# A transformer block with three branches on one core: TensorE's list tied to the order of the source

## The chip, the cores and the metric

The kernel runs on one core of one Trainium2 chip. A core has five engines with a list of instructions each: TensorE (PE; its weight loads are shown as PEld), VectorE (DVE), ScalarE (ACT), GpSimd (POOL) and SyncE (SP), which issues most transfers. The metric is device microseconds of one execution of the program, as the median of several runs.

## The reference

One block over 512 tokens of 1,024 channels, in float32. A modulation of `c` scales and shifts both norms and gates both residuals. The first half projects the normed input to three mixing branches of 512 channels and to three gates:

```python
mod = cond @ w_ada[l] + b_ada[l]
h = rms_norm(x) * norm1_g[l] * (1.0 + sc1) + sh1
proj = h @ w_in[l]
...
y_fox = fox_attention(...)      # softmax attention with a decay from cumulative log gates
y_hgrn = hgrn2_branch(...)      # linear attention with data-dependent decay, chunks of 64
y_rwkv = rwkv7_branch(...)      # delta rule: state S, then S*w - (S k)(k a) + v k, token by token
merged = (g_fox * (y_fox @ w_branch[l, 0]) + g_hgrn * (y_hgrn @ w_branch[l, 1])
          + g_rwkv * (y_rwkv @ w_branch[l, 2]))
x = x + gt1 * (merged @ w_out[l])
h = rms_norm(x) * norm2_g[l] * (1.0 + sc2) + sh2
u = causal_dwconv(h @ w_up[l], conv_w[l], conv_b[l])
x = x + gt2 * ((silu(u_gate) * u_val) @ w_down[l])
```

## The kernel before, in words

**Stages.** The kernel has a start (first modulation parts, the first norm, the first tiles of `w_in`), an interleaved part (all projections, the three branches, the gates and the merge), the output product with the second norm, and the FFN (`w_up`, convolution, `w_down`).

**Large products.** Each float32 weight tile is split into a high and a low part, and a product is three matmuls of the type float32r (`mm3`, L348): high x high, high x low, low x high. `load` (L337 for the transfer) fetches 256 KB, and `split` puts the high part on ScalarE (L329) and the low part on VectorE or GpSimd (L330). The raw tiles have 3 buffers, the parts 6 each. A product's output has one of 3 PSUM banks (`mm`), the branches' small products share 5 more (`br`).

**Streams.** In the interleaved part seven generators take turns, in this order of precedence: `rwkv_b`, `rwkv_a`, `hgrn`, `foxes`, `prep`, `ada_stream` and `big`. Each branch works in four groups of two heads. `big` is a list of jobs with the large weights, one `mm3` for each of eight blocks of rows between two yields. A step of a stream ends with `yield lat`. The planner `run` keeps a clock, `clk`, that counts an estimated TensorE time for each matmul and transpose from its shape alone, and a stream may go on when `clk` has passed its last `lat` times 0.9, plus 1.65. At each turn the first stream in the list that is due makes its next step; `need` and `post` hand results from one stream to another with a due time. So the source's order of matmuls follows from shapes and from these constants.

**The framework's order.** The kernel is written in a framework that works out tiles' places, semaphores and each engine's list by itself. It goes through the traced instructions with a model of time: an instruction is put on its engine's list when the model has its operands and buffers ready, earlier ones of the source first among those that are ready. So an instruction that the model holds to be late is overtaken by later ones. Each engine then runs its list in order. `tc.issue_after(ins)` says that what is traced in the block comes behind `ins` on the same engine's list; it orders the issue and does not wait for the end of `ins`. Two accesses to one PSUM tile by different engines, one of them a write, are ordered by semaphores even where the columns differ.

**The places that matter here.**
- `rwkv_b` (L985 on) is a chain over 8 chunks for each of the four groups, in one PSUM tile per chunk. A chunk has three steps: the product with `G` and `MV` (columns 0 to 63) and its copy `xst` (L1001); the product of `Z64` and `xst` (64 to 127) and `UV` from it (L1010); and the last step, in which, for c < 7, the product `BT x UV` (128 to 191) is read by two VectorE instructions into the next `MV` (L1020, in chunk 0 L1023), and then the output products `AR x MV` and `G x UV` (192 to 255) are read by ScalarE (L1031).

```python
            if c < 7:
                for hh in range(2):
                    mm(ps[HS[hh], 128:192], BT[hh][:, c, :], uv[:, hh, :])
...
                for hh in range(2):
                    hs = HS[hh]
                    if c > 0:
                        v.scalar_tensor_tensor(out=mvn[hs, hh, :], in0=ps[hs, 128:192], scalar=wc[hs, c:c + 1],
                                               in1=xst[hs, cl, 1, :], op0=ALU.mult, op1=ALU.add)
...
            for hh in range(2):
                hs = HS[hh]
                o = ps[hs, 192:256]
                if c > 0:
                    mm(o, AR[hf][hs, cl, 1, :], mv[hs, hh, :], True, False)
                mm(o, G[hh][hf][:, cl, 64:128], uv[:, hh, :], c == 0, True)
```

- `split2` (L465 ScalarE, L466 VectorE) makes two parts `shi` and `slo` of a float32 tile. `rwkv_a` calls it in the head of the loop that multiplies both by `bonesr` (four times), and `ada_stream` in the one that multiplies both by `onesr` (four times).
- `rwkv_a` waits for a spread reciprocal norm `rnx` (L438) before four transposes, and multiplies `AR` by `BK` in four groups of four.
- `fox_decay` makes the first product of the interleaved part (tile `wf`).
- `transpose` and `mm` are the two helpers that every stream calls; most matmuls therefore have L88 and most transposes L92.

Of the kernel before, what the change touches and what calls it, by code (L numbers as in the profile page):

```python
# [42 lines left out]
def block_kernel(ctx: ExitStack, tc: tile.TileContext, I, out, dbg=None, upto=99):  # L43
# [32 lines left out]

    # the work of the branches is cut in steps, which the streams below interleave; the clock counts the work of the
    # tensor engine, and a step says after how much of it the operands of the next are expected
    clk = [0.0]

    def mm(o, lhsT, rhs, start=True, stop=True):
        n = rhs.free_size() if hasattr(rhs, "free_size") else math.prod(rhs.shape[1:])
        if rhs.dtype == F32R:
            clk[0] += n / 2400
        else:
            half = (0.5 if lhsT.shape[0] <= 64 else 1.0) * (0.25 if math.prod(lhsT.shape[1:]) <= 32 else 1.0)
            clk[0] += half * max(0.17, n / 600)
        return pe.matmul(o, lhsT=lhsT, rhs=rhs, start=start, stop=stop)  # L88

    def transpose(o, i, idn):  # L90
        clk[0] += 0.11 if i.shape[0] > 64 else 0.07
        pe.transpose(o, i, idn)  # L92

# [14 lines left out]
    def run(streams):  # L108
        """streams in the order of their precedence"""
        live = [[gen, 0.0, False] for gen in streams]  # L110
        while live:
            done = False
            for st in live:
                if st[1] > clk[0] + 1e-9:
                    continue
                c0, n0 = clk[0], len(avail)
                try:
                    lat = next(st[0])
                except StopIteration:
                    live.remove(st)  # L120
                    done = True
                    break
                if lat is None and c0 == clk[0] and n0 == len(avail):
                    continue
                lat = lat or 0.0
                st[1] = clk[0] + (lat * LAT[0] + LAT[1] if lat else 0.0)
                done = True
                break
            if not done:
                later = [st[1] for st in live if st[1] > clk[0] + 1e-9]  # L130
                assert later, "streams wait for each other"
                clk[0] = min(later)
# [16 lines left out]

    # ---------------------------------------------------------------- constants  # L150
    con = cp.tile([P, NCONST], F32, name="con")
    lmask = cp.tile([P, 5, 64], I32, name="lmask")
    last = {}

    def behind(key, emit):
        """an instruction queued behind the one before with the same key"""
        if key in last:
            with tc.issue_after(last[key]):
                r = emit()
        else:  # L160
            r = emit()
        last[key] = r.ins
        return r
# [49 lines left out]

    # ---------------------------------------------------------------- x, modulation
    modc = cp.tile([P, 48], F32, name="modc")
# [57 lines left out]

    # ---------------------------------------------------------------- norm helpers
    def rstd_of(ss, n, eps, dst, w):
# [24 lines left out]
    def normed(xs):  # L300
        """the normed halves of a tile of 128 tokens"""
        return norm_scale(xs, norm_stats(xs))
# [18 lines left out]

    # ---------------------------------------------------------------- weights
    nld = [0]
# [20 lines left out]
    def load8(src, c0):  # L344
        """1024 x 128 of a weight, in two halves; the parts of each block of 128 rows"""
        return load4(src, c0, 0) + load4(src, c0, 1)
# [5 lines left out]

    # the first tiles of w_in take the first half of the channels while the second is on its way
    ALLT = list(range(4))
# [54 lines left out]
    def chunk_tokens(src, dst):  # L409
        """channels x tokens to tokens x channels: chunks of 64 tokens, odd heads in the other half of the partitions;  # L410
        dst(hh, par) takes the chunks 2 * i + par"""
        ps = PSB()
# [8 lines left out]
    def chunk_channels(src):  # L421
        """the inverse of chunk_tokens: (head, parity of the chunk, [64 channels, 4 chunks, 64 tokens])"""
        ps = PSB()
# [17 lines left out]
    def head_bcast(rnx):  # L441
        """[128 tokens, (tile, head)] to a PSUM bank [128 channels, 512 tokens]"""
        psr = PSB()
# [4 lines left out]
    def head_sums(sqs, sums=None):  # L448
        """of each [128 channels, 512 tokens] the sums over the channels of a head, as [128 tokens, (tile, head)]"""
        n = len(sqs) * P  # L450
# [17 lines left out]

    # ================================================================ HGRN
    lbm = small("lbm", [P, 4])  # L470
# [11 lines left out]
    def hgrn(gi):  # L482
# [23 lines left out]
        for li, m in enumerate(LEVELS):  # L506
            ps = PSB()
            for c in range(8):
                for hh in range(2):
                    if m == 32:  # L510
                        # the lower half of the chunk against the upper one only
                        qq = Q[2 * hh + c % 2]
# [20 lines left out]
        vi, = yield from need(("hi", gi))  # L533
        # [A; q] and [V; state] of each head, odd heads with the halves exchanged: one product takes both
        VM = [T2("VM", [P, 8, 64]) for _ in range(2)]
# [64 lines left out]

    # ================================================================ FOX
    ncum = dp.tile([6, 8, 512], F32, name="ncum")
# [6 lines left out]
    def fox_decay():  # L609
# [23 lines left out]
        v.tensor_tensor_scan(out=cum, data0=one, data1=z, initial=0.0, op0=ALU.mult, op1=ALU.add)  # L633
        # the sum in three parts, and their negatives
        for i in range(3):
# [14 lines left out]
    def fox(gi):  # L650
# [9 lines left out]
        g.tensor_tensor(out=rn, in0=rn, in1=as3(neghalf[:, 0:16], 8), op=ALU.pow)  # L660
        # [high; low] of q against [high; high] of k (odd heads: [low; high]), and high of q against low of k with the
        # parts of the sums of both tokens
        A = [[T2("qk1", dt=F32R) for _ in range(2)] for _ in range(2)]
# [81 lines left out]

    # ================================================================ RWKV
    w2s = []
# [29 lines left out]
    def rwkv_evac(n, j, ps):  # L777
# [11 lines left out]
        if n == "rwa":  # L789
            # [high; low] parts, for products with [high; high] and with the low part of the weights  # L790
            ll = []
# [20 lines left out]
    def rwkv_a(gi):  # L812
# [64 lines left out]

        # products of all pairs of steps in a chunk, for both heads
        G, BT = [[None, None], [None, None]], []
        Ld = T2("Ld", [P, 8, 64])  # L880
        for hf in range(2):
            for hh in range(2):
# [7 lines left out]
                yield 0.0  # L890
        # inverses of the 16 x 16 diagonal blocks, one system (chunk, head, block) per partition
        d1 = dp.tile([8 * 8320], F32, tag="d1", bufs=2, name=nm("d1"))
# [34 lines left out]
        for x in range(2):  # L927
            sync.dma_start(d2[x].rearrange("(s e) -> s e", e=256), XZ[:, x].rearrange("p i j -> p (i j)"))
            sync.dma_start(Xc[:, x], dview(d2, x * 8 * 2048, [[16, 128], [2048, 8], [1, 16]]))
        # [U; V] and [state; V] of each chunk: odd heads have the halves exchanged  # L930
        UV = [T2("UV", [P, 4, 2, 64]) for _ in range(2)]
# [44 lines left out]
        for hh in range(2):  # L976
            v.tensor_scalar(out=Z64[Q[2 * hh], :, 32:64], in0=ps[Q[2 * hh], 0:256].rearrange("p (c j) -> p c j", j=32),
                            scalar1=-1.0, scalar2=0.0, op0=ALU.mult, op1=ALU.add)
            for hf in range(2):
                # the rows of the inverted block give way to alpha: one product then takes the state and V  # L980
                s.activation(G[hh][hf][HS[hh], :, 0:64], AR[hf][HS[hh], :, 0, :], AF.Copy)
# [3 lines left out]
    def rwkv_b(gi):  # L985
# [47 lines left out]
        post(("chained", gi), None)  # L1033
        # group norm over the 64 channels of each head
        sm = small("gsum", [P, 8])
# [26 lines left out]

    # ================================================================ products with the large weights
    gt1 = [T2("gt1") for _ in range(2)]
# [74 lines left out]
    def ada_stream():  # L1139
        """the rest of the modulation, on engines that have time left"""  # L1140
        yield 100.0
# [80 lines left out]
    def foxes():  # L1222
        yield from fox_decay()
        yield from each(fox)

    run([each(rwkv_b), each(rwkv_a), each(hgrn), foxes(), prep(), ada_stream(), big(jobs)])

# [53 lines left out]

    # ================================================================ FFN
    cw_rows = T2("cw_rows", [44, 4, 128])
# [13 lines left out]

    # the first tiles start with the first half of the tokens, while the norm of the second is worked out
    begun = []
# [39 lines left out]
    for k in range(KT):  # L1339
        for q in range(2):  # L1340
            w = load(w_down, k * P, P, q * 512, 512)
            for tt in range(4):
                down_mm(k, q, tt, w)
    # the last rows tile by tile, so that the tiles are done one after the other
    ws = [[load(w_down, k * P, P, q * 512, 512) for k in range(KT, 22)] for q in range(2)]
# [9 lines left out]

# [1 line left out]
def _constants(np):  # L1357
# [5 lines left out]
    m = np.where(rho, sp <= tp, sp < tp).astype(np.float64)  # L1363
    # without the products of the steps of a block of 16, whose inverse is worked out apart
    off = (i[:, None] % 64) // 16 != (i[None, :] % 64) // 16
# [45 lines left out]
```

## Time and profile before

| what | us |
|---|---|
| median of 3 runs | 1149.66 |
| the 3 runs | 1149.66, 1147.6, 1160.29 |
| the profiled execution | 1160.29 |
| its span, from the first to the last instruction | 1158.6 |
| TensorE busy in the span | 1111.0 (96%) |
| VectorE, ScalarE, GpSimd busy | 697.9, 520.8, 302.7 |

The profile is of one execution. Start times are microseconds from the span's first instruction. Matmuls are pipelined, so that one 128x512 matmul shows some 0.39 us though the next one starts 0.23 us after it; what counts is the distance between starts. A float32 matmul shows as two records, so the count of a small product in a row is twice that in the source. "Idle before" stands in square brackets with what ended it.

### The profile page before, as it was taken

What the parts mean: (1) busy time and instruction counts of PE and PEld (TensorE: products, weight loads), DVE (VectorE), ACT (ScalarE), POOL (GpSimd) and SP (SyncE); (2) the same over time, 40 slices, a digit from 0 to 9 for tenths busy, and PEclk for the clock granted to TensorE, in tenths of its full rate; (3) what the DMA queues carried; (4) which work ended last, traced back from release to release, by engine and by line L of the source; (5) the groups of instructions that cost most, each with busy time, mean ns of one, the idle gap of its engine ahead of it and who ended that gap; (6) DMA issues with size and microseconds to landing.
All of it is one profiled execution on the core that took longest, in us unless ns stands there. A gap on an engine that the chain in (4) does not pass through costs nothing. (4 is left out here: it accounts for less than half of the span.)

```text
span 1158.6 us, 19335 instructions
## 1 busy us (share of the span) xinstructions
PE 1111.0 (96%) x7297; PEld 858.9 (74%) x7297; DVE 697.9 (60%) x1477; ACT 520.8 (45%) x975; POOL 302.7 (26%) x322
## 2 busy tenths in 40 slices
PE   4998999999999999999999999899999999999998
PEld 2567876777777776677767888688888888888886
DVE  1567668777688778676653824735666666661114
ACT  2475575256535653568432434323444444442220
POOL 3015424323343234231131622432101101101110
PEclk9999999899999998999989999899999999999999
DMA  9633352133412413143524455301333333333332
GB/s 312 200 77 78 79 141 57 40 107 77 129 31 85 118 48 112 38 110 101 154 56 127 112 178 173 119 1 32 109 98 95 99 95 98 99 94 97 100 98 84
DMA packets 175475, 117.60 MB, mean 102 GB/s; under 512 B 25360, under 2 KB 151350, under 8 KB 175382
## 3 DMA queue, kind: packets, MB, share of 16 engines
q1 hardware_dynamic: 173696, 116.22, 35.0%
q8 instruction: 57, 0.93, 0.3%
q14 instruction: 36, 0.29, 0.1%
q10 hardware_dynamic: 1238, 0.12, 0.1%
q0 software_dynamic: 448, 0.03, 0.0%
HBM read 112.57 MB, written 3.77 MB: 100 GB/s over the span
## 5 line engine op out<-in xcount | busy, mean ns | idle before, releaser
L329 ACT ACTIVATE whi<-raw 128x512 fp32r<-128x512 f32 x282 | 176.1, 629 | 351.9 <-PE mm L88 230.3
L330 DVE TENSOR_TENSOR wlo<-raw,whi 128x512 fp32r<-128x512 f32 x212 | 151.4, 715 | 153.1 <-ACT whi L329 152.2
L330 POOL TENSOR_TENSOR wlo<-raw,whi 128x512 fp32r<-128x512 f32 x70 | 94.9, 1355 | 460.3 <-ACT whi L329 436.0
L88 PE MATMUL mm<-hhi,whi 128*128 128x512 f32 x504 | 212.5, 422 | 0.3 <-DVE rwa L780 0.3
L88 PE MATMUL mm<-hhi,wlo 128*128 128x512 f32 x504 | 202.6, 402 | 0.0
L88 PE MATMUL mm<-hlo,whi 128*128 128x512 f32 x504 | 202.2, 401 | 0.0
L88 PE MATMUL mm<-h2hlo,whi 128*128 128x512 f32 (+1 forms) x376 | 141.5, 377 | 1.2 <-POOL h2hlo L1261 1.2
L88 PE MATMUL mm<-h2hhi,whi 128*128 128x512 f32 (+1 forms) x376 | 141.3, 376 | 0.0
L88 PE MATMUL mm<-h2hhi,wlo 128*128 128x512 f32 (+1 forms) x376 | 141.2, 376 | 0.0
L88 PEld LDWEIGHTS mm<-hhi,whi 128*128 128x128 f32 x504 | 96.7, 192 | 24.0 <-issue 2.0
L88 PEld LDWEIGHTS mm<-hhi,wlo 128*128 128x128 f32 x504 | 96.5, 191 | 21.7 <-issue 0.4
L88 PEld LDWEIGHTS mm<-hlo,whi 128*128 128x128 f32 x504 | 96.7, 192 | 16.7 <-issue 0.4
L88 PEld LDWEIGHTS mm<-h2hlo,whi 128*128 128x128 f32 x376 | 70.7, 188 | 14.7 <-POOL h2hlo L1261 2.0
L88 PEld LDWEIGHTS mm<-h2hhi,wlo 128*128 128x128 f32 x376 | 70.7, 188 | 12.9
L88 PEld LDWEIGHTS mm<-h2hhi,whi 128*128 128x128 f32 x376 | 70.7, 188 | 12.9
L1319 DVE SCALAR_TENSOR_TENSOR u<-mm,cw,u 128x511 f32<-128x511 f32 x44 | 32.8, 746 | 54.7 <-ACT u L1318 54.7
L1150 DVE SCALAR_TENSOR_TENSOR adac<-ada,cs,adac 128x512 f32<-128x512 f32 x56 | 45.1, 805 | 0.7
L1004 POOL TENSOR_SCALAR xst<-MV,wc 64x64 f32<-64x64 f32 x48 | 20.8, 434 | 93.7 <-DVE MV L1020 86.0
L88 PE MATMUL br<-wlo,ahi 128*128 128x512 f32 x110 | 42.8, 389 | 0.0
L88 PE MATMUL br<-whi,alo 128*128 128x512 f32 x110 | 42.8, 389 | 0.0
L88 PE MATMUL br<-whi,ahi 128*128 128x512 f32 x110 | 42.8, 389 | 0.0
L88 PE MATMUL mm<-yhi,whi 128*128 128x512 f32 x96 | 38.7, 404 | 0.7 <-DVE gt L1130 0.7
(385 smaller groups left out, 2026.4 us busy)
## 6 DMA issues: line engine op xcount, KB each, us to landing
raw<-in_w_in_dram SPq DMA_DIRECT2D x126, 256.0 KB
ada<-in_w_ada_dram SPq DMA_DIRECT2D x96, 256.0 KB
raw<-in_w_up_dram SPq DMA_DIRECT2D x88, 256.0 KB
raw<-in_w_down_dram SPq DMA_DIRECT2D x44, 256.0 KB
raw<-in_w_branch_dram SPq DMA_DIRECT2D x24, 256.0 KB
wo<-in_w_out_dram SPq DMA_DIRECT2D x16, 256.0 KB
x<-in_x_dram SPq DMA_DIRECT2D x8, 256.0 KB
mg<-in_x_dram SPq DMA_DIRECT2D x8, 256.0 KB
```

The lines of the kernel that those rows point to most:

```text
L88: return pe.matmul(o, lhsT=lhsT, rhs=rhs, start=start, stop=stop)
L329: s.activation(hi, raw, AF.Copy)
L330: (g if leng == "g" else v).tensor_tensor(out=lo, in0=raw, in1=hi.bitcast(F32), op=ALU.subtract)
L1004: g.tensor_scalar(out=xst[HS[hh], cl, 1, :], in0=mv[HS[hh], hh, :], scalar1=wc[HS[hh], c:c + 1], scalar2=0.0, op0=ALU.mult, op1=ALU.add)
L1150: v.scalar_tensor_tensor(out=acc, in0=raws[k], scalar=cs[:, k:k + 1], in1=acc, op0=ALU.mult, op1=ALU.add)
L1319: v.scalar_tensor_tensor(out=u[:, 1:], in0=ps[:, :511], scalar=cw[:, 1, jj:jj + 1], in1=u[:, 1:], op0=ALU.mult, op1=ALU.add)
```

## The change

`mm` and `transpose` pass their instruction through `in_order`, which remembers the last one and, once the flag `strict` is set, traces the next inside `tc.issue_after` of it. The flag is set right before the interleaved part starts and isn't set back, so the products of `w_out` and the FFN that go through `mm` are tied too; the transposes of the norms (L311) and of the convolution's weights call `pe.transpose` directly and are not. Apart from that the diff removes comments, which moves the line numbers.

```diff
+    pe_last = [None]
+
+    def in_order(emit):
+
+        if pe_last[0] is None or not strict[0]:
+            r = emit()
+        else:
+            with tc.issue_after(pe_last[0]):
+                r = emit()
+        pe_last[0] = r.ins
+        return r
+
+    strict = [False]
...
     def mm(o, lhsT, rhs, start=True, stop=True):
...
-        return pe.matmul(o, lhsT=lhsT, rhs=rhs, start=start, stop=stop)
+        return in_order(lambda: pe.matmul(o, lhsT=lhsT, rhs=rhs, start=start, stop=stop))
 
     def transpose(o, i, idn):
         clk[0] += 0.11 if i.shape[0] > 64 else 0.07
-        pe.transpose(o, i, idn)
+        in_order(lambda: pe.transpose(o, i, idn))
...
+    strict[0] = True
     run([each(rwkv_b), each(rwkv_a), each(hgrn), foxes(), prep(), ada_stream(), big(jobs)])
```

## Rows read from the trace of the kernel before

**Rows 1.** The page's busy times of the whole span, with shares and counts.
```profile
PE 1111.0 (96%) x7297; PEld 858.9 (74%) x7297; DVE 697.9 (60%) x1477; ACT 520.8 (45%) x975; POOL 302.7 (26%) x322
```

**Rows 2.** Busy us by stretch: PE, PEld, DVE, ACT, POOL (x instructions), clock, DMA share, GB/s.
```profile
54.40:736.00 681.60, 659.80 (x5228) 495.72 (x5228) 465.04 (x1100) 348.96 (x678) 226.65 (x234) 0.97 0.36 98
811.00:1141.00 330.00, 330.00 (x1457) 273.05 (x1456) 166.81 (x244) 127.14 (x207) 38.80 (x30) 1.00 0.33 96
```

**Rows 3.** TensorE's waits: us in total, times, longest us.
```profile
PE br L88 <- POOL pr L492: 3.0, 1, 3.0
...
PE br L88 <- DVE MV L1020: 2.3, 2, 1.7
```

**Rows 4.** The tile MV: ns min/median/max, first and last start.
```profile
L1020 DVE SCALAR_TENSOR_TENSOR MV<-br,wc,xst x48: 265/284/292, 199.3 to 625.7; 64x64 f32<-64x64 f32 x48
...
L1023 DVE TENSOR_SCALAR MV<-br,wc x8: 249/284/292, 190.3 to 559.7; 64x64 f32<-64x64 f32 x8
```

**Rows 5.** Timeline from 245.9 us: start, us, engine, line, operation, tiles, count.
```profile
246.03 0.28 PE L88 MATMUL br<-UV,BT 128*64 128x64 f32 x4
...
246.25 0.91 PE L88 MATMUL br<-VM,ktok 64*64 64x64 f32 x22
246.43 0.60 DVE L1020 SCALAR_TENSOR_TENSOR MV<-br,wc,xst 64x64 f32<-64x64 f32 x2 [2.12 <-PE br L88]
...
247.09 0.33 PE L88 MATMUL br<-MV,AR 64*64 64x64 f32 x2
```

**Rows 6.** Timeline, TensorE and VectorE, at 188.9 and at 589 us.
```profile
188.93 0.34 PE L88 MATMUL br<-UV,BT 128*64 128x64 f32 x4
...
190.31 0.57 DVE L1023 TENSOR_SCALAR MV<-br,wc 64x64 f32<-64x64 f32 x2
...
589.42 0.34 PE L88 MATMUL br<-UV,BT 128*64 128x64 f32 x4
...
592.15 0.60 DVE L1020 SCALAR_TENSOR_TENSOR MV<-br,wc,xst 64x64 f32<-64x64 f32 x2
```

**Rows 7.** TensorE's timeline at 101 and 463 us; L466's VectorE instructions.
```profile
101.42 0.40 PE L88 MATMUL mm<-hhi,whi 128*128 128x512 f32 x1
...
109.39 0.49 PE L88 MATMUL br<-slo,bonesr 128*128 128x512 f32 x1
...
463.26 0.80 PE L88 MATMUL mm<-hhi,whi 128*128 128x512 f32 x1
...
471.80 0.50 PE L88 MATMUL br<-slo,bonesr 128*128 128x512 f32 x1
...
L466 DVE TENSOR_TENSOR slo<-rk,shi x4: 681/686/874, 108.4 to 471.0; 128x512 fp32r<-128x512 f32 x4
```

**Rows 8.** TensorE's timeline from 80 us, with the idle time before the last.
```profile
80.61 0.39 PE L88 MATMUL mm<-hhi,whi 128*128 128x512 f32 x1
...
84.46 0.39 PE L88 MATMUL mm<-hhi,wlo 128*128 128x512 f32 x1
86.17 0.66 PE L92 MATMUL br<-con,rnx 128*128 128x128 f32 x4 [1.32 <-DVE rnx L438]
```

**Rows 9.** TensorE's timeline from 92 us.
```profile
92.14 0.39 PE L88 MATMUL mm<-hhi,whi 128*128 128x512 f32 x1
...
94.67 2.82 PE L88 MATMUL br<-AR,BK 64*128 64x128 f32 x32
```

**Rows 10.** Busy us by stretch around stalls, with the granted clock (columns as in rows 2).
```profile
208.50:210.70 2.20, 0.03 (x3) 0.03 (x2) 2.13 (x6) 0.14 (x1) 0.70 (x1) 1.00 0.00 0
210.90:221.10 10.20, 10.20 (x78) 8.26 (x75) 5.65 (x12) 1.84 (x5) 1.47 (x3) 0.50 0.19 30
453.30:466.90 13.60, 13.04 (x79) 9.76 (x80) 8.48 (x23) 5.04 (x14) 1.95 (x4) 0.50 0.17 26
593.20:600.00 6.80, 6.80 (x22) 4.82 (x22) 1.18 (x3) 0.85 (x2) 0.46 (x1) 0.50 0.16 41
```

## The prediction

> **What bounds the kernel now.** I read the page's busy shares first, then the busy times by stretch, then TensorE's list of waits, then the timeline at the places that the change touches. TensorE is busy for 96% of the span, VectorE for 60% [rows 1]. From its first instruction of the interleaved part at 54.4 us to the last at 736 us TensorE is busy 659.80 of 681.60 us: 21.8 us are idle [rows 2]. VectorE has 465 us of work there, so no other engine comes near. The longest single wait in the part's list is 3.0 us, for POOL's `pr`; two for VectorE's `MV` make 2.3 together [rows 3]. So the part ends when TensorE has got through its list. Its work is the same before and after the change: the time moves only by idle time that is added or taken away, and by the clock.
>
> What keeps idle time so low is the framework's reordering. Setting the order that the planner's source gives beside the order in the trace, about 1,100 of some 3,700 matmuls and transposes of the part stand elsewhere, most by under 30 places, one by 116. Nearly always it is one pattern: a small product whose operand is late is overtaken by the three-product groups of a large weight. After the change nothing overtakes, so TensorE stands where it now fills.
>
> **The change, part by part.** It removes and adds no instruction, and it orders issue without waiting for an end. Everything behind the waiting matmul on TensorE's list waits with it: the other streams' small products, the large weights' groups, and through these the splits on ScalarE that need a weight buffer back and the next weight loads on SP's queue. None of these is late by itself; they get TensorE's delay.
>
> *Chain steps of `rwkv_b`.* In each of the steps c < 7 the source has the product `BT x UV` into columns 128 to 192 of a PSUM tile, two VectorE instructions that read them (L1020, or L1023 in step 0), and at once, without a yield, the output products into columns 192 to 256 of the same tile. 48 and 8 VectorE instructions, two a step, make 28 places [rows 4]. The output products need only `UV`, which is there, but they wait for `MV`: the list has two such waits, the longer 1.7 us [rows 3], at the places where too little else stood ready. Where VectorE is free, the `BT` product starts at 246.03, `MV` takes 246.43 to 247.03, the output products start at 247.09; in between TensorE did 11 products of another stream, from 246.25 on [rows 5]. Without these it would stand from 246.25 to 247.09, 0.84 us. 28 x 0.84 = 23.5 us. That is the floor of this term, as an instruction on VectorE can't be skipped.
>
> In ten of the 28 places VectorE comes late, 0.9 to 4.6 us after the `BT` product, the first at 190.31 behind a row of scans, the last at 592.15 behind two `adac` updates [rows 6]; together 20.5 us, or 19.5 over the prompt case. With TensorE standing, less new work reaches VectorE, but chains like these scans go on. I take 6, with 0 and 19.5 as the ends.
>
> *Products of parts just split* (L904, L1161). `split2` is called in the loop's head, with ScalarE and VectorE work and the product of it in one step. For `bonesr` the trace has four such, and TensorE did other things from the source's place to the second part's product: 101.42 to 109.39 in the first, 463.26 to 471.80 in the last [rows 7], 5 to 6 us in the two between. For `onesr` three of four are delayed, by 1 to 4 us. All of it would be 33 us. Most will not come: ScalarE's `shi` stood behind weight splits that waited for large products, which now stand behind `bonesr`, so the framework must put `shi` first. What then remains is one activation and one subtraction; the subtraction takes 0.69 us [rows 7], so some 1.4 us for both if nothing is done ahead. 7 x 1.4 = 10 at most, 0 if both parts are done in time; I take 8.
>
> *The first streams.* From 80.61 to 84.69 TensorE did 18 large products ahead of the transposes of `rnx`, and stood for 1.32 us all the same [rows 8]: 4.1 us more of standing. From 92.14 ten more overtook the products `AR x BK` until 94.67 [rows 9]: 2.3 us. Together 6.4; the decay product of `fox`, 20 places earlier in the source's order, brings its VectorE work forward, so `rnx` may come sooner. I take 5, ends 0 and 6.4.
>
> *The rest of the overtaking*, around 320 to 360 and 460 to 490 us, fills places between chain steps. I take 2, ends 0 and 7: at most 29 large products stand ahead of their place there, at 0.23 us each (17 steps from 80.61 to 84.46 [rows 8]).
>
> *The clock.* TensorE was idle from 208.5 to 210.7, and then the granted clock was 0.50, that is 1.2 of 2.4 GHz, for 10.2 us; the same level follows stalls at 453.3 for 13.6 us and at 593.2 for 6.8 us [rows 10]. Half of each is lost, 15.3 us in all now. Standing under a microsecond at a time need not bring it; the long ones above may. One more such stretch costs 3.4 to 6.8. I take +4, ends -15 and +25.
>
> *Absorbed.* While TensorE stands at a new place, the engines that cause the 21.8 us of present idle time run ahead. I take 8 of it as gone, ends 0 and 17.
>
> Sum: 23.5 + 6 + 8 + 5 + 2 + 4 - 8 = 40.5 us. The terms are from one execution, 1160.29 us with a span of 1158.6; it is the slowest of the three shown, and 10.6 over their median. The sum for it is 1200.8; set on the median of 1149.66 it is 1190 us. FFN and the output product are tied too, as the flag is not set back, but the trace's order there is the source's almost throughout, and I count nothing.
>
> The Trainium skill (Perfetto Trace Analysis, Identifying the Most-Contended Engine) speaks against reading the bound from matmul busy time: it would have the busy share of the weight loads looked at. That share is 72.7% in the interleaved part against 82.7% in a stretch of FFN [rows 2], so by this rule TensorE has a tenth of the part to spare, and the delays could vanish in it. That is the second rival below; the small products load narrower weights, so I don't read the whole difference as room.
>
> **The rivals.**
> 1. *Faster: the present stalls go.* If the source's order, which was planned for operands in time, avoids the stalls after which the clock halves, the most to win is 21.8 us of idle time [rows 2] and 15.3 us of clock [rows 10]; a third of it, with nothing new to pay, gives 1137. It decides if the 28 places cost under 0.3 us each. Against it: `MV` alone takes 0.60 us at each [rows 5], and the stall at 208.5 stands where the order hardly differs.
> 2. *No change: TensorE has slack.* The new standing replaces the old, and the engines behind it catch up: 23.5 less 17 and less one half-clock stretch gives 1151. For it: the weight loads' share. Against it: the late operands depend on TensorE's own earlier products, so they move along.
> 3. *The change hardly does anything*, as seven in ten products are in place already. It would show as 28 places still filled; 1150. The source ties each one to the one before, so I see no way.
> 4. *Much slower: the clock breaks.* VectorE late at all ten places, half the 33 us of the split parts, and four or five more half-clock stretches: 43 + 17 + 6 + 10 + 20 - 5 = 91, so 1241.
>
> **How the numbers follow.** The forecast, slower by 16 to 80 us, has 0.77; rival 1 0.04; rivals 2 and 3 together 0.10; rival 4 0.09. A change under 1%, 11.5 us, is about what a measurement can't tell from none. The low end: 23.5 + 4 + 3 - 14 = 16.5, so 1166. The high end: 43 + 12 + 6 + 6 + 18 - 5 = 80, so 1230. Faster 0.04, within 1% 0.10, slower 0.86.
>
> **What would show it.** In the profile after: the list of TensorE's waits led by VectorE's `MV`, some 28 of them, 0.7 us or more each and 23 to 43 us in total; waits for `slo` and `rnx`; idle time of 55 to 80 us in the part in place of 21.8; the busy time of FFN unchanged; VectorE's busy time unchanged. It is wrong if the waits for `MV` total under 12 us, if the part's idle time does not grow, or if the growth sits in half-clock stretches and not in waits.

## The result and the profile after

The changed kernel takes 1221.64 us (median of 4 runs, 1218.75 to 1222.82) against 1152.94 us for the kernel before (4 runs on the same chip, 1147.6 to 1160.29): a ratio of 1.0566, 95% interval 1.0519 to 1.0612. It is 68.7 us slower by the medians. The two profiled executions, on which the accounting below rests, differ by less, since the one of before was the slowest of its four: their spans are 1219.3 and 1158.6 us, 60.7 us apart.

The page's busy times after, to be set beside [rows 1]:

```profile
PE 1125.8 (92%) x7297; PEld 874.6 (72%) x7297; DVE 697.1 (57%) x1477; ACT 520.6 (43%) x974; POOL 299.3 (25%) x322
```

TensorE issues the same 7297 matmuls, and no other engine has more work. TensorE's share fell from 96 to 92%, and its busy time rose by 14.8 us, though nothing was added to its list. So the loss has two parts: idle time, and the same work done more slowly.

The busy times by stretch show where, with the columns of [rows 2]. The first line is the interleaved part, from the same first instruction at 54.4 us to the same last one, now at 795.0 us; the second is a stretch of FFN.

```profile
54.40:795.00 740.60, 674.07 (x5203) 511.59 (x5201) 462.16 (x1092) 347.65 (x676) 223.16 (x234) 0.93 0.33 90
870.00:1200.00 330.00, 329.89 (x1460) 273.03 (x1459) 167.02 (x244) 128.25 (x208) 39.06 (x31) 1.00 0.33 97
```

The part grew from 681.6 to 740.6 us, by 59.0; only 1.7 of the 60.7 us lie outside it. Of the 59.0, 44.7 us is idle time (740.60 less 674.07 is 66.5; it was 21.8), and 14.3 us is busy time (674.07 less 659.80). The mean granted clock of the part fell from 0.97 to 0.93. FFN is as it was.

TensorE's waits after (us in total, times, longest us) answer to [rows 3]:

```profile
PE br L102 <- DVE MV L1034: 37.2, 24, 6.1
...
PE br L106 <- DVE rnx L452: 4.2, 3, 2.1
PE br L102 <- DVE MV L1037: 4.0, 4, 1.7
PE br L102 <- DVE slo L480: 3.7, 5, 1.5
...
PE br L102 <- POOL pr L506: 3.0, 1, 3.0
PE br L102 <- DVE UV L1024: 2.4, 2, 1.9
PE br L102 <- ACT shi L479: 2.3, 2, 1.5
```

`MV` leads with 24 and 4 waits, 28 in all and 41.2 us, where it had two and 2.3 us. `slo` and `shi` are new, with 6.0 us. Three lines of before that are not in [rows 3] show what changed little or went:

```profile
PE br L92 <- DVE rnx L438: 3.2, 3, 1.4
...
PE br L88 <- DVE mx L707: 2.0, 1, 2.0
PE br L88 <- POOL qk L686: 1.9, 3, 1.0
```

`rnx` rose by 1.0 us, `mx` left the list, `pr` and `UV` stand as they stood.

The next two fences are timelines after (start, us, engine, line, operation, tiles, count, idle time before and what ended it). The first is a place at which VectorE is free, to be set beside [rows 5]; the second is the longest wait.

```profile
268.31 0.28 PE L102 MATMUL br<-UV,BT 128*64 128x64 f32 x4
...
268.71 0.60 DVE L1034 SCALAR_TENSOR_TENSOR MV<-br,wc,xst 64x64 f32<-64x64 f32 x2 [3.02 <-PE br L102]
...
269.37 0.33 PE L102 MATMUL br<-MV,AR 64*64 64x64 f32 x2 [0.77 <-DVE MV L1034]
```

```profile
393.30 0.63 PE L102 MATMUL br<-VM,ktok 64*64 64x64 f32 x16
...
393.86 0.34 PE L102 MATMUL br<-UV,BT 128*64 128x64 f32 x4
...
394.75 0.69 DVE L344 TENSOR_TENSOR wlo<-raw,whi 128x512 fp32r<-128x512 f32 x1 [2.14 <-ACT whi L343]
...
395.47 0.48 DVE L569 COPY VM<-br 64x64 f32<-64x64 f32 x2
395.98 3.72 DVE L573 SCALAR_TENSOR_TENSOR VM<-VM,fts,br 64x64 f32<-64x64 f32 x12
399.62 0.59 DVE L1034 SCALAR_TENSOR_TENSOR MV<-br,wc,xst 64x64 f32<-64x64 f32 x2
...
400.27 0.47 PE L102 MATMUL br<-MV,AR 64*64 64x64 f32 x2 [6.07 <-DVE MV L1034]
```

In the first, the two `BT` products (four records) are followed on TensorE by nothing at all until both `MV` instructions are through: 0.77 us idle, where before 11 products of another stream stood (22 records) [rows 5]. In the second, the `BT` products are over at 394.2, but VectorE stands in its own queue's order: first for a split that waits for ScalarE, then through it, two copies and twelve updates of `VM`, and only then `MV`. TensorE waits 6.07 us. The 28 waits are 15 of 0.70 to 0.95 us and 13 longer ones, from 1.01 to 6.07.

### The profile page after: what moved, and what is told of

The parts are those of the page before. It is cut to its first block, busy times and chain, and to the rows that moved or that the text cites. A ratio compares the mean times of both kernels' runs of the same rounds, so it can differ in the third digit from the quotient of the medians.

```text
span 1219.3 us, 19342 instructions
## 1 busy us (share of the span) xinstructions
PE 1125.8 (92%) x7297; PEld 874.6 (72%) x7297; DVE 697.1 (57%) x1477; ACT 520.6 (43%) x974; POOL 299.3 (25%) x322
## 5 line engine op out<-in xcount | busy, mean ns | idle before, releaser
L102 PE MATMUL mm<-hhi,whi 128*128 128x512 f32 x504 | 219.8, 436 | 0.1
L102 PE MATMUL mm<-hlo,whi 128*128 128x512 f32 x504 | 204.9, 407 | 0.0
L102 PEld LDWEIGHTS mm<-hhi,whi 128*128 128x128 f32 x504 | 99.6, 198 | 26.7 <-issue 3.9
L102 PEld LDWEIGHTS mm<-hhi,wlo 128*128 128x128 f32 x504 | 99.2, 197 | 22.9
L102 PEld LDWEIGHTS mm<-hlo,whi 128*128 128x128 f32 x504 | 99.9, 198 | 16.0
L102 PE MATMUL br<-MV,AR 64*64 64x64 f32 x112 | 19.5, 258 | 37.2 <-DVE MV L1034 37.2
L1045 ACT ACTIVATE ot<-br 128x64 f32<-128x64 f32 x32 | 7.1, 222 | 85.6 <-PE br L102 85.4
L1018 POOL TENSOR_SCALAR xst<-MV,wc 64x64 f32<-64x64 f32 x48 | 19.5, 406 | 96.3 <-DVE MV L1034 88.4
L102 PEld LDWEIGHTS br<-MV,AR 64*64 64x64 f32 x112 | 11.4, 142 | 44.2 <-DVE MV L1034 40.6
```

Source lines behind the costliest of these rows:

```text
L102: return in_order(lambda: pe.matmul(o, lhsT=lhsT, rhs=rhs, start=start, stop=stop))
L1018: g.tensor_scalar(out=xst[HS[hh], cl, 1, :], in0=mv[HS[hh], hh, :], scalar1=wc[HS[hh], c:c + 1], scalar2=0.0, op0=ALU.mult, op1=ALU.add)
L1045: s.activation(ot[:, c, :], ps[:, 192:256], AF.Copy)
```

## The experiments

The kernel before was timed again beside each group of runs, each group on another chip; the ratios are to it. Its medians were 1155.17 us (the first four runs), 1158.08 (the next four), 1158.77 (the three after) and 1159.26 (the last), so a few microseconds between runs of different groups are best read from the ratios. The half-clock times given below are added up from the trace's granted-clock records of 0.50 between 60 and 1140 us: 41.0 us in 5 stretches for the kernel before, 109.2 us in 16 for the changed one.

**The 28 places: take their wait away in two ways.** The first run puts the output products ahead of the `BT` products in the source; all is tied. So they come before VectorE begins to read the tile.

```diff
+            for hh in range(2):
+                hs = HS[hh]
+                o = ps[hs, 192:256]
+                if c > 0:
+                    mm(o, AR[hf][hs, cl, 1, :], mv[hs, hh, :], True, False)
+                mm(o, G[hh][hf][:, cl, 64:128], uv[:, hh, :], c == 0, True)
             if c < 7:
                 for hh in range(2):
                     mm(ps[HS[hh], 128:192], BT[hh][:, c, :], uv[:, hh, :])
...
-            for hh in range(2):
-                hs = HS[hh]
-                o = ps[hs, 192:256]
...
```

> Everything stays tied as in the changed kernel, but in the source the output products of a chunk stand ahead of the product BT x UV, so nothing that TensorE does next waits for VectorE's MV. Theory 1 (the 28 waits for MV, 41.2 us, are most of the loss, and the half-clock stretches that come with them the rest): the list has no waits for MV, or some of them under 3 us in total, idle time in the interleaved part falls from 66.6 to some 30 us, and the time from 1221.6 to 1165 to 1180. Theory 2 (TensorE is late everywhere once nothing overtakes; the waits for MV only show where): other waits, for UV, xst, slo, rnx, grow by 20 us or more and the time stays above 1200.

The second leaves the order and gives the output products a PSUM tile of their own.

```diff
+            pso = PSB()
             for hh in range(2):
                 hs = HS[hh]
-                o = ps[hs, 192:256]
+                o = pso[hs, 192:256]
...
-            s.activation(ot[:, c, :], ps[:, 192:256], AF.Copy)
+            s.activation(ot[:, c, :], pso[:, 192:256], AF.Copy)
```

> TensorE's order is exactly the changed kernel's, but the output products of a chunk go into a PSUM tile of their own. Theory 1 says that the wait is for the shared tile alone, not for a value: the waits for MV go though each output product still follows BT x UV directly, and the time falls to 1165 to 1180, as in the run with another order. Theory 2: under 20 us come back. If PSUM gets short (a tile more out of 5), waits for the readers of the br tiles rise instead by up to 10 us.

They took 1186.69 us (ratio 1.027, 1.0222 to 1.0318) and 1186.17 us (1.027, 1.0219 to 1.032). Both give back 35 us of the loss, less than the 42 to 57 expected (1165 to 1180 us). From the second run's waits:

```profile
PE br L102 <- DVE slo L480: 9.9, 6, 4.7
...
PE br L106 <- DVE rnx L452: 5.3, 4, 2.6
PE br L102 <- DVE xst L1015: 4.9, 3, 2.7
PE br L102 <- ACT shi L479: 3.3, 3, 1.5
...
PE br L102 <- DVE MV L1034: 3.0, 1, 3.0
```

`MV` fell from 41.2 to 3.0 us. That another PSUM tile alone does it shows that the wait comes from sharing the tile, not from needing `MV`. The Trainium skill (PSUM — Partial Sum Buffer, Summary: rules for kernel authors) has it that matmuls go to another bank while one is being read; the run shows what that was worth here, 35 us for 28 places. But about 31 us of loss stay, and the waits for other late operands grew: `slo` from 3.7 to 9.9, `xst` from 1.7 to 4.9. With the large wait gone the stream meets the next late operand, and nothing fills that either. The half-clock time fell only from 109.2 to 88.7 us in the first run and to 81.9 in the second, so it does not hang on the waits for `MV` alone.

**The 28 places alone.** The third run is the kernel before, with nothing tied but these places: whatever the source has after the output products stays behind them, and they stay behind the `BT` products.

```diff
+    bar = [None]
+
+    def behind_bar(emit):
+        if bar[0] is None:
+            return emit()
+        with tc.issue_after(bar[0]):
+            return emit()
...
-                    mm(ps[HS[hh], 128:192], BT[hh][:, c, :], uv[:, hh, :])
+                    bar[0] = mm(ps[HS[hh], 128:192], BT[hh][:, c, :], uv[:, hh, :]).ins
...
-                mm(o, G[hh][hf][:, cl, 64:128], uv[:, hh, :], c == 0, True)
+                r = mm(o, G[hh][hf][:, cl, 64:128], uv[:, hh, :], c == 0, True)
+                if c < 7:
+                    bar[0] = r.ins
```

> The kernel before, with only the 28 places tied: an output product directly behind BT x UV, and whatever follows in the source behind it; between these places the framework reorders as before (half as many products out of place). Theory 1: waits for MV of 35 to 45 us, and 1195 to 1210, that is 40 to 57 us of the 69. Theory 2: the waits show, but other idle time shrinks for them, and the time is under 1175.

The fourth is its mirror: the changed kernel, with the 28 groups of output products untied.

```diff
+        if loose[0]:
+            return pe.matmul(o, lhsT=lhsT, rhs=rhs, start=start, stop=stop)
         return in_order(lambda: pe.matmul(o, lhsT=lhsT, rhs=rhs, start=start, stop=stop))
...
+            loose[0] = c < 7
             for hh in range(2):
...
+            loose[0] = False
```

> The changed kernel with only the output products of the 28 places left untied. Theory 1: 1165 to 1185, idle time near 30 us; what is left over the kernel before (12 to 32 us) is the split parts, the first streams and the clock. Theory 2: above 1200.

Alone, the 28 places make 1199.94 us (ratio 1.0393, 1.0333 to 1.0453), 45 us over before. The waits of that run reproduce those of the changed kernel almost to the tenth:

```profile
PE br L95 <- DVE MV L1027: 37.1, 24, 5.7
...
PE br L95 <- DVE MV L1030: 4.0, 4, 1.7
PE br L99 <- DVE rnx L445: 3.4, 3, 1.5
...
PE br L95 <- POOL pr L499: 3.0, 1, 3.0
```

Freed, they give 1190.58 us (1.0314, 1.0256 to 1.0373), 31 us less than the changed kernel and short of the 1165 to 1185 us expected; `slo` rises to 10.7 us there. So these places are worth 31 to 45 us of 68.7, by whether they are taken out of the whole or put in alone. The two differ because the time saved goes in part to the next wait, and because in the third run nothing else can move across the 28 places either, so that 45 is an upper figure for them.

**Products of parts just split.** Here only the products that read the halves made by `split2` are untied, first in the kernel with the output products first, then in the changed kernel itself (`loose` as above).

```diff
+        loose[0] = True
         for i, part in enumerate(split2(rk)):
             mm(psk, bones, part, i == 0, i == 1)
+        loose[0] = False
```

> The order of e1 (output products ahead of the BT products), and only the ten-odd products that take a part just split by VectorE (bones with the two halves of r*k, onesr with the halves of the head average) are left untied; everything else stays tied. Theory A (what is left of the loss in e1, 31 us, is many small waits of TensorE on VectorE, each no longer filled): the waits named slo and shi, 5.6 + 3.0 us in e1, fall to under 2 us, and the time falls by 6 to 9 us from e1's, to about 1178 us. Theory B (the small waits also pull the clock down, and the half-clock time costs as much again): the time falls by 10 to 18 us, to about 1172 us, and the half-clock time falls from e1's 89 us to about 70. Theory C (the waits only move: the next late operand ends the same stretch): waits of the same size appear under rnx, xst or UV and the time stays within 3 us of e1's 1187.

> The changed kernel, with only the products that take a part just split by VectorE (bones and onesr) untied; all the rest is tied, the shared tile's waits included. Theory A: slo and shi, 3.7 + 2.3 us in the changed kernel, go; the waits for MV stay at about 41 us; the time falls by 4 to 6 us to about 1216 us. Theory B (with the clock): by 8 to 14 us, to about 1210 us. Theory C (the waits only move): within 3 us of 1221.

The first took 1178.9 us (ratio 1.0192, 1.0136 to 1.0248), 7.8 us under the run that it starts from; the second 1215.86 us (1.0519, 1.0469 to 1.0568), 5.8 us under the changed kernel. `slo` and `shi` fell from 8.6 to 4.3 us and from 6.0 to 2.5 us, not to nothing, and the half-clock time by 7 and 14 us. By the times Theory A is the nearest: the term is about 6 us. It is not paid as waits alone: the busy time of the second profiled execution is 1122.4 us against 1125.8, so that 3.4 of the 6.0 us between the two spans are busy time.

**Filling the wait with work that nobody reads.** Into each of the 28 places of the changed kernel come three products whose result nothing uses; the wait itself stays. Nothing else is changed; TensorE has 84 matmuls more.

```diff
+            if c < 7:
+                idle = PSB()
+                for _ in range(3):
+                    in_order(lambda: pe.matmul(idle, lhsT=onesr, rhs=hhi[:, 0, :], start=True, stop=True))
             for hh in range(2):
```

> The changed kernel, and at each of the 28 places three products of 128x512 that nobody reads are put between the BT products and the output products, tied there (the work added is 84 products, about 84 x 0.22 = 18 us at full clock, and lies where TensorE stood waiting about 0.9 us a place). Theory 1 with the clock (a good part of the loss is half-clock time that follows the waits): the waits named MV fall from 41 us to some 20 to 25 us, since TensorE works through part of each; the half-clock time falls from 109 us toward 75, and the kernel gets faster, by 5 to 15 us, although it does more work: about 1211 us. Theory 1 without the clock (the loss is the waits alone, and the half-clock time does no harm of its own): the products fill the waits and nothing else changes, so the time stays within 4 us of 1221. Rival (the products run past the eviction's end and hold up the stream behind them): 3 to 10 us slower.

It took 1210.83 us (ratio 1.0471, 1.042 to 1.0521): 10.8 us *faster* than the changed kernel, with more to do. Its page and its wait for `MV`:

```profile
PE 1134.4 (94%) x7381; PEld 877.3 (73%) x7381; DVE 697.4 (58%) x1477; ACT 520.3 (43%) x974; POOL 299.3 (25%) x322
```

```profile
PE br L102 <- DVE MV L1034: 15.5, 10, 5.2
...
PE br L102 <- DVE MV L1037: 0.8, 1, 0.8
```

`MV` fell from 41.2 to 16.3 us. The span less the busy time fell from 93.5 to 70.8 us, by 22.7. The busy time rose by 8.6 us, although 84 products at a step of 0.23 us each (as in [rows 8]) are 19.3 us more work; so the old work took about 10.7 us less. Half-clock time fell from 109.2 to 68.3 us. If the added work had only filled time that was lost anyway, the time would have stayed. Less half-clock time is the one thing seen to change that fits the gain, and the time came out as expected on that ground; no run holds the clock still, so its share isn't isolated. The clock is then a cost of its own that comes with the waits.

**The order in the source, with nothing tied.** The kernel before with the output products first, as in the first run.

> The kernel before, with the output products placed ahead of the BT products in the source and nothing tied. Theory 1 (before the change other work fills the shared tile's wait, so the place in the source costs next to nothing): the waits named MV, 2.3 us before, go, and the time is within 4 us of before's 1153. Rival (the place in the source already cost the kernel before something through its chain, since the output products hold the next MV up by nothing but the fillers do): 5 to 10 us faster. Second rival (the output products now stand ahead of BT on the chain to the next MV, about 0.3 us a passage of 28, 8 us): up to 8 us slower.

1153.95 us over 12 runs, ratio 0.9985 (0.9959 to 1.0012): no difference. `MV` is off the list, and it doesn't matter, since these waits were filled. The same edit that gives the tied kernel 35 us gives the untied one nothing.

**Which tie it is.** The products of the big projections (`mm3`, 128x512 each) are untied, and all products and transposes of the branches stay tied to one another, but for the one product in each group of `rwkv_b` that also goes through `mm3`; then the mirror, with only what goes through `mm3` tied.

```diff
     def mm3(ps, lh, ll, rh, rl, first, last):
+        loose[0] = True
         mm(ps, lh, rh, first, False)
         mm(ps, lh, rl, False, False)
         mm(ps, ll, rh, False, last)
+        loose[0] = False
```

> The changed kernel, and the 128x512 products of the big projections (three to a step of mm3) are left untied; every product and transpose of the branches stays tied behind the one before it of the branches. Theory 1 (what the tie takes away is that a projection product which is ready is pulled into a wait; which branch product comes after which matters little): the waits named MV fall from 41 us to under 8 us, the half-clock time from 109 us toward the 41 us of before, and the time to 1155 to 1170 us. Theory 2 (the branches need one another's products as fillers, since their own order is what waits): MV keeps over 20 us and the time stays above 1190 us.

> The mirror of e9: in the changed kernel only the 128x512 products of the big projections are tied, each step of mm3 behind the one before it, and every product and transpose of the branches is untied. Theory 1: the branches can still move against the projections, so this is the kernel before but for the order among projection products, which came in their order there too: within 6 us of before's 1155 us, waits named MV under 5 us. Theory 2 as in e9 gives the same here, so this run tells whether the tie as such (its semaphores, its place in the program) costs anything: if it does, over 1165 us with no wait of over 2 us to show for it.

With the projections free: 1151.44 us over 10 runs (before 1158.77 over 25), ratio 0.9956, 0.9925 to 0.9987. With only the projections tied: 1159.65 us, ratio 1.0023, 0.9992 to 1.0054. The whole loss is gone in both. The 0.44% of the first is no gain at the same clock: nine of its ten executions have a mean granted clock of 0.986 to 0.990 and take 1148.3 to 1155.5 us, and the 17 of 62 executions of the kernel before with such a clock take 1148.4 to 1153.4, while its other 45, at 0.977 to 0.984, take 1155.2 to 1163.1. The waits of the first:

```profile
PE br L109 <- DVE rnx L457: 3.4, 3, 1.4
...
PE br L105 <- POOL pr L511: 3.0, 1, 3.0
PE br L105 <- DVE MV L1039: 2.9, 4, 1.7
```

This settles it. In this run the branch products still come in the source's order, the output products still wait for `MV` at all 28 places, and VectorE is still late: at one of them, the timeline shows four projection products started between a first and a second `MV` instruction that are 0.9 us apart:

```profile
198.59 0.28 DVE L1039 SCALAR_TENSOR_TENSOR MV<-br,wc,xst 64x64 f32<-64x64 f32 x1
198.67 0.39 PE L104 MATMUL mm<-hlo,whi 128*128 128x512 f32 x1
...
198.90 0.39 PE L104 MATMUL mm<-hhi,wlo 128*128 128x512 f32 x1
...
199.13 0.39 PE L104 MATMUL mm<-hhi,whi 128*128 128x512 f32 x1
...
199.35 0.39 PE L104 MATMUL mm<-hlo,whi 128*128 128x512 f32 x1
199.48 0.29 DVE L1039 SCALAR_TENSOR_TENSOR MV<-br,wc,xst 64x64 f32<-64x64 f32 x1
...
199.83 0.32 PE L105 MATMUL br<-MV,AR 64*64 64x64 f32 x2
```

What the change took away is not the framework's order of the branches but the freedom of the projection products and the branches to move against each other. Ties as such cost nothing: the mirror has the waits of before (`MV` 2.3, `mx` 2.0, `rnx` 3.2 us) and its 41.0 us of half-clock time.

**Both kernels beaten.** The untied projections with the output products first, and then with the tile of their own.

> e1 (output products ahead of the BT products) with the 128x512 products of the big projections untied, as in e9. Theory 1 for the 31 us that e1 still loses (many small waits that no projection product may fill): slo, shi, xst, nmx and MV together fall from e1's 22 us to under 8 us, the half-clock time from 89 us to under 60, and the time to within 8 us of before's 1155 us. Rival (the branches' own order, one branch product held up behind another branch's late operand, makes the small waits): they stay above 15 us and the time above 1172 us.

> e2 (output products in a PSUM tile of their own) with the 128x512 products of the big projections untied, as in e9 and e11. If e11's 1 per cent over the kernel before comes from taking the output products off the wait for MV, this run has the same gain: a ratio of 0.987 to 0.993, with no wait named MV of over 1 us in all. If it comes from e11's own order (output products first, BT products later), this one stays at e9's ratio of 0.996. If the 28 tiles more a pass crowd the other users of the same PSUM buffers, it is slower than e9: over 0.998, with new waits for a tile's release.

1146.53 us over 10 runs, ratio 0.99 (0.987 to 0.993), and 1146.93 us over 8, ratio 0.9913 (0.9879 to 0.9947). Both are about 1% faster than the kernel before, and here not by the clock: the first run's executions, at 0.975 to 0.987, take 1141.5 to 1148.6 us, the kernel before at 0.977 to 0.990 never under 1148.4. The waits of the first:

```profile
PE br L109 <- DVE rnx L457: 4.2, 4, 1.4
...
PE br L105 <- POOL pr L511: 3.0, 1, 3.0
PE br L105 <- DVE xst L1020: 2.2, 2, 1.7
...
PE br L105 <- DVE mx L726: 2.0, 1, 2.0
```

`MV`, `slo` and `nmx` are gone; the 40 us between this run and the tied one (1186.69) are the projection products alone. That the second has the same gain as the first says that the gain over the 0.9956 comes from taking the output products off the wait, whichever way; in the kernel before, untied, the same edit gained nothing. Where inside the 12 us that part of it sits isn't settled: the span less the busy time of the page is 46.9 us against 47.6 before and the half-clock time 41.0 in both, so it is busy time, 1099.3 against 1111.0. Busy time can thus differ by 11.7 us at the same half-clock time.

## Why the prediction came out as it did

The direction was right with its mechanism: the part's end moves by idle time that nothing fills and by the clock, and the time, 1221.64, lies in the range of 1166 to 1230, in its upper part. The forecast of 1190 was short by 31.6 us, as it was set on a median of 1149.66; on the profiled executions, from which its terms were read, it was short by 18.5 (40.5 against the 59.0 by which the part grew). Term by term:

| term | forecast | measured | from |
|---|---|---|---|
| Chain steps, the floor | 23.5 | 21.6 | 28 x 0.77 |
| Chain steps, VectorE late | 6 | 19.6 | 41.2 less 21.6 |
| Products of parts just split | 8 | 6.0 | `slo` 3.7, `shi` 2.3 |
| The first streams | 5 | 1.0 | `rnx` 4.2 less 3.2 |
| The rest of the overtaking | 2 | 2.7 | other small waits: `kt` 1.5, `xst`, `lst`, `XZ` 0.4 each |
| The clock | 4 | 14.3 | busy time of the part, all of it put down to the clock |
| Absorbed | -8 | -6.2 | what is left to 44.7 us of idle time |

*The floor* was right in count and nearly in size: 28 places, 0.77 us where VectorE is free against 0.84 reckoned from [rows 5].

*VectorE late* is the term that was mis-sized first. The prediction had the bound right (19.5 from the ten late places of [rows 6]) and then took 6, because "with TensorE standing, less new work reaches VectorE". In sum it does not come down: 13 places are over 1 us, and their lateness comes to the upper end, 19.6. That it comes so near is partly luck: taken place by place, the ten that were late before bring 15.1 of it, one of them being prompt now, and four that were prompt before bring 4.4. The place at 394 us shows why so much stays. What VectorE has to do ahead of `MV` there is not new work from TensorE but a queue already handed out, with a split that itself waits for ScalarE and the updates of `VM`, whose products TensorE started at 393.30, ahead of `BT`. A late operand priced from the trace should have been kept at its measured lateness unless a row shows the work ahead of it going away.

*The clock* is the second. The prediction let waits under a microsecond be harmless and thought of the long ones as few, one more stretch or so. But 13 of the new waits are longer, and half-clock time went from 41.0 us in 5 stretches to 109.2 in 16. Four of the stretches, by the columns of [rows 2]:

```profile
222.60:232.80 10.20, 9.33 (x75) 8.40 (x76) 4.39 (x10) 1.36 (x4) 1.47 (x3) 0.50 0.26 53
366.00:383.00 17.00, 15.52 (x117) 11.41 (x117) 9.07 (x31) 5.56 (x14) 1.93 (x3) 0.50 0.10 14
396.70:406.90 10.20, 6.63 (x34) 4.89 (x35) 3.42 (x13) 0.50 (x2) 0.64 (x2) 0.50 0.09 25
529.80:540.00 10.20, 9.43 (x71) 6.66 (x69) 4.97 (x21) 3.10 (x7) 2.90 (x4) 0.50 0.12 30
```

The first begins within the 2.40 us wait that ends at 223.47, the second 0.5 us after a wait of 3.54, the third inside the one of 6.07 shown above, the fourth 0.9 us after a wait of 1.67 for `xst`. Eleven waits for `MV` are 1.34 us or longer, and ten of the sixteen stretches begin in one of them or within 2.2 us of its end. The prediction had the price of a stretch and the right row to see it; it lacked that most of the new stretches begin at the long waits that its lateness term made too few. Other late operands bring them as well, as the two runs with a single wait for `MV` left show (88.7 and 81.9 us of half-clock time). Its upper end for the clock, 25, holds what came. But 14.3 is the growth of busy time, and by the run with both changes (11.7 us less at the same half-clock time) not all of such a difference need be the clock's, so the size of the term stays open.

*Products of parts just split* was near: 6.0 us listed, and 5.8 us given back when they alone are untied. *The first streams* was too high by 4: the standing at `rnx` grew by 1.0 us only, though the 18 large products no longer stood ahead of it. The prediction's reservation, that `rnx` may come sooner, is what the trace shows: the transposes that wait for it start 4.0 us sooner than at 86.17 [rows 8].

```profile
82.17 0.66 PE L106 MATMUL br<-con,rnx 128*128 128x128 f32 x4 [2.13 <-DVE rnx L452]
```

What made `rnx` come sooner was not tested. The measured *rest of the overtaking* is a sum of small waits, of which `kt` (117 us) and `lst` (62 us) lie outside the two places that the prediction had in mind; its 2.7 for 2 is no confirmation. *Absorbed* was nearly right: `MV`'s own 2.3 us, `mx` and part of `qk` went.

Of the rivals, 4 is the nearest: it named the two terms that ran high, VectorE late at every place (43 us for the chain steps; 41.2 came) and the clock (20; 14.3 came), and overshot with the split parts (17; 6.0 came) and the small terms. Rival 2, that TensorE has slack, falls. The weight loads' share, which carried it by the Trainium skill (Perfetto Trace Analysis, Identifying the Most-Contended Engine), is 69.1% of the part after (511.59 of 740.60) against 72.7%. There was room in that sense, but it was no room for delay, as the operands that are late hang on TensorE's own products; and it took free projection products, not slack, to bring the time back. Rival 3, that the change hardly does anything, is refuted by 28 of 28 places standing open. Rival 1, that the source's order would remove stalls, is wrong for the change and has a grain that the runs bring out: with the projections free and the branches in the source's order, nine of ten executions have the higher granted clock that 17 of 62 have before, and the profiled one has 13.7 us of half-clock time. The order that the planner gives the branches is no worse than the framework's; the loss comes only from fixing the projections against it.

What the prediction said of *what would show it* held: `MV` in the lead with 28 waits, 41.2 us within its 23 to 43, waits for `slo` and `rnx`, idle time of 66.5 us within its 55 to 80, VectorE and FFN unchanged. It was named as wrong if the growth sat in half-clock stretches and not in waits; it sat in waits to three quarters.

## What to carry to other kernels

Where one engine runs at 96% through many chains, most waits are real and are only covered: before an order is fixed, count the places where something else stands in the trace between a product and the eviction that shares its tile, and price each at its full lateness, not at the prompt case. If an order has to be fixed, fix it among the dependent small products, or among the large independent ones, and leave the two free against each other; here that is the difference between 5.7% slower and no loss (ratios 0.9956 and 1.0023). A tile shared by two products with an eviction between them costs nothing in the kernel before, where other products fill the wait, and 35 us once they can't.

## What the runs showed that was not expected

The prediction had no place for it, though the run's own expectation did: work that nobody reads can make the kernel faster. 84 added products took 10.8 us off, as TensorE stood for `MV` at 11 places instead of 28 and half-clock time fell from 109.2 to 68.3 us. And busy time moves with half-clock time, by less than was reckoned. The same 7297 matmuls have these busy times in the run with the projections free, which has 13.7 us of half-clock time:

```profile
PE 1094.6 (95%) x7297; PEld 849.0 (74%) x7297; DVE 705.9 (62%) x1477; ACT 525.4 (46%) x979; POOL 304.5 (27%) x322
```

They were busy for 1111.0 us before, with 41.0 us of it, and for 1125.8 us after, with 109.2 us. From before to after 68.2 us more of half-clock time go with 14.8 us more of busy time, a fifth; from the run with the projections free 95.5 us go with 31.2, a third; in the run with the added products it was 10.7 for 40.9, a quarter. The prediction put half on each stretch. For the large products that is near: in the stretch from 82.7 us on, at a granted clock of 0.50, they start 0.43 us apart, against 0.23 at the full clock [rows 8].

```profile
83.48 0.63 PE L102 MATMUL mm<-hhi,wlo 128*128 128x512 f32 x1
83.91 0.63 PE L102 MATMUL mm<-hhi,whi 128*128 128x512 f32 x1
```

Part of the difference is that the stretches hold idle time (3.6 of 10.2 us at 396.7). And the busy time isn't the clock's alone: it differs by 11.7 us between the kernel before and the run with the projections free and the output products first, both with 41.0 us of half-clock time. The rest is open.
